# Two decoder layers on one core: the last of the eight squares of a norm kept beside the sum of the other seven, and added behind the transposes

## The chip, the cores and the metric

One core of a Trainium2 chip runs the whole program. The metric is the device time of one execution in microseconds. Lower is better.

## The reference, cut to what matters

Two layers of a decoder trunk work on x of 256 tokens by 1024 channels in float32. Each layer begins its two halves with an RMSNorm over the channels:

```python
def _rms(x, g):
    xf = x.astype(jnp.float32)
    y = xf * lax.rsqrt(jnp.mean(xf * xf, axis=-1, keepdims=True) + EPS)
    return (y * g.astype(jnp.float32)).astype(x.dtype)

xn = _rms(x, norm_mix_g);  z = einsum(xn, w_in)     # three mixers and their gates
x = x + einsum(merged, w_out)
xn = _rms(x, norm_ffn_g);  g, u = split(einsum(xn, w_gate_up))
x = x + einsum(silu(g) * u, w_down)
```

So there are four norms in the program: mixer and feed-forward of the first layer, then mixer and feed-forward of the second.

## The kernel before, in words

x lies transposed, as eight tiles x[0] to x[7] of 128 channels by 256 tokens. Every large product takes its operands as a sum of two parts, hi and lo (xg, fx, h, mg and y for activations, whi and wlo for weights), and is made of three matmuls (`feat`: hi by hi, hi by lo, lo by hi). The weights arrive in chunks of up to 128x1024 by DMA into raw. ScalarE makes whi from raw, VectorE makes wlo; there are three buffers of each.

`norm` does not scale x by its root mean square. It gives out the parts of x times the gain at once, and beside them the inverse root mean square in two shapes: rcol (tokens on the partitions) and rB (tokens along the free axis, the same on each partition). The products run on the unscaled parts, and their results are multiplied with rcol or rB when they leave PSUM. The PSUM tiles of the products (mm) have four buffers, those of all else (at) four more.

The sum of squares in `norm`, before: ScalarE squares x[0] into nacc and x[1] to x[7] into work tiles nsq, and GpSimd adds each nsq to nacc, seven adds in a row. In the first norm of the program, where x comes from memory, ScalarE squares all eight tiles into one wide tile sq and VectorE halves it three times (1024, 512 and 256 columns), the last time into nacc. Then two TensorE transposes (one for each half of the tokens, identity K1 as the moving operand) put nacc into a PSUM tile 128x2x128, VectorE reduces that over the channels to rcol (128x2), scales it and adds EPS, GpSimd takes the power -0.5 (rsqrt_cols), VectorE spreads rcol into rc, four transposes turn rc into PSUM, and ScalarE copies the result to rB. `S.gang()` keeps the transposes of a group together on TensorE and makes the first of them wait for all that the group needs.

The order of all instructions comes from a planner inside the kernel (`Order`). Every operation is recorded with a cost (`cost`, `lat`), and `Order.schedule` lays them out engine by engine in simulated time, by their place in the program and by when their inputs are ready. Each engine then runs its own list in that order. The costs that matter here:

```python
    if op.eng == "gpsimd":
        ...
        return 0.15 + n * 0.0021
```

and 0.2 us of latency to or from GpSimd. Work tiles (tag w) share 15 buffers. `Order.issue` first places the tags that PLACED names, in its order, with spaces in bytes between them; what follows nacc there (xg, y, h, w, mqk, K1) lies behind it in SBUF. In the trace every recorded instruction has the line 323 (`getattr(...)(*args, **kw)` in `Order.issue`), so instructions are told apart by their tiles.

Of the kernel before, what the change touches and what calls it, by code (L numbers as in the profile page):

```python
# [11 lines left out]
F32 = mybir.dt.float32  # L12
F32R = mybir.dt.float32r
BF16 = mybir.dt.bfloat16
AF = mybir.ActivationFunctionType
OP = mybir.AluOpType
AX = mybir.AxisListType.X
# [100 lines left out]
class Order:  # L118
# [191 lines left out]
    def issue(self):  # L310
        nc = self.tc.nc
        self.makespan = self.schedule()
        for tag in PLACED:
            if isinstance(tag, int):
# [79 lines left out]
T = 256  # L394
# [18 lines left out]
BR = (1, 2, 0)  # L413


PLACED = ("whi", "wlo", "nacc", 192, "xg", "y", "h", 192, "w", 224, "mqk", 192, "K1", 416)


def plan():
# [37 lines left out]
def kernel(ctx: ExitStack, tc: tile.TileContext, xT: bass.AP, wts: bass.AP, cst: bass.AP,  # L457
# [6 lines left out]
    S = Order(tc, sbuf, psum)  # L464
    V, A, G, PE, SP = (S.engine(n) for n in ("vector", "scalar", "gpsimd", "tensor", "sync"))

    def mmps(shape):
        return S.tile(shape, F32, tag="mm", name="mm", bufs=4, psum=True)

    def atps(shape):  # L470
        return S.tile(shape, F32, tag="at", name="at", bufs=4, psum=True)

    def tmp(shape, name="w"):
        return S.tile(shape, F32, tag="w", name=name, bufs=NW)
# [6 lines left out]
    K1 = S.tile([128, 256], F32, name="K1")  # L481
# [4 lines left out]
    x = [xs[:, 8 + k * T:8 + (k + 1) * T] for k in range(8)]  # L486
    ident, ones = K1[:, 0:128], K1[:, 128:256]
# [21 lines left out]
    def chunk(li):  # L509
        i = widx[0]  # L510
        widx[0] += 1
        w = WIDTH[i]
        raw = S.tile([128, CH], F32, tag="raw", name="raw", bufs=3)
        hi = S.tile([128, CH], F32R, tag="whi", name="whi", bufs=3)
        lo = S.tile([128, CH], F32R, tag="wlo", name="wlo", bufs=3)
        src = wts[li, OFFS[i]:OFFS[i + 1]].rearrange("(p c) -> p c", p=128)
        with S.early(600):
            if li == 0 and i < 2:
                return raw, hi, lo, src
            SP.dma_start(raw[:, :w], src)  # L520
            split(raw, hi, lo, 0, w)
        return hi, lo
# [20 lines left out]
    def rsqrt_cols(t, n):  # L543

        G.tensor_tensor(t, t, mhalf[:, :n], op=OP.pow)

    def gained(a, k, g):
        A.activation(a[:, 0, :], x[k], AF.Copy, scale=g)
        V.scalar_tensor_tensor(a[:, 1, :], x[k], g, a[:, 0, :].bitcast(F32), op0=OP.mult, op1=OP.subtract)

    def norm(gcol, wide, xg=None):

        first = xg is not None
        xg = xg or []
        acc = S.tile([128, T], F32, tag="nacc", name="nacc")
        for k in range(8 - len(xg)):
            g = gcol[:, k:k + 1]
            if not wide:
                a = S.tile([128, 2, T], F32R, tag="xg", name="xg", bufs=8)
            else:  # L560
                if k % 4 == 0:
                    y4 = S.tile([128, 4, 2, T], F32R, tag="y", name="fx", bufs=3)
                a = y4[:, k % 4]
            gained(a, k, g)
            xg.append(a)
        if first:
            sq = S.tile([128, 8 * T], F32, tag="y", name="sq8", bufs=3)
            with S.after(w_first[1][1]):
                for a in (0, 4 * T):
                    A.activation(sq[:, a:a + 4 * T], xs[:, 8 + a:8 + a + 4 * T], AF.Square)  # L570
            for n in (4 * T, 2 * T):
                V.tensor_add(sq[:, 0:n], sq[:, 0:n], sq[:, n:2 * n])
            V.tensor_add(acc, sq[:, 0:T], sq[:, T:2 * T])
        else:
            for k in range(8):
                if k == 0:
                    A.activation(acc, x[k], AF.Square)
                else:
                    sq = tmp([128, T], "nsq")
                    A.activation(sq, x[k], AF.Square)  # L580
                    G.tensor_add(acc, acc, sq)
        ps = atps([128, 2, 128])
        with S.gang():
            for t in range(2):
                PE.transpose(ps[:, t, :], acc[:, t * 128:(t + 1) * 128], ident)
        rcol = S.tile([128, 2], F32, tag="rcol", name="rcol", bufs=2)
        V.tensor_reduce(rcol, ps, axis=AX, op=OP.add)
        V.tensor_scalar(rcol, rcol, 1.0 / D, EPS, op0=OP.mult, op1=OP.add)
        rsqrt_cols(rcol, 2)
        rr = tmp([128, 2, 128], "rc")  # L590
        V.tensor_copy(rr, rcol[:, :, None].to_broadcast([128, 2, 128]))
        ps = atps([128, 2, T])
        with S.gang():
            for i in range(2):
                for t in range(2):
                    PE.transpose(ps[:, i, t * 128:(t + 1) * 128], rr[:, t, :], ident)
        rB = S.tile([128, T], F32, tag="rB", name="rB", bufs=2)
        A.activation(rB, ps[:, 0, :], AF.Copy)
        return xg, rcol, rB
# [161 lines left out]
    for li in range(L):  # L761
        widx[0] = 2 if li == 0 else 0
        c = col[li]
        r = row[li] = S.tile([128, R_N], F32, tag="row", name="row")
        ps_first = mmps([128, 2, T]) if li == 0 else None
        if li == 0:
            first_pair(ps_first)
        xg, rcol, rB = norm(c[:, C_NM:C_NM + 8], False, xg0 if li == 0 else None)
        if li:
            SP.dma_start(r, rows[li:li + 1, :].to_broadcast([128, R_N]))  # L770
# [6 lines left out]
        mqk = []  # L777
        for fp in range(4):
            if li == 0 and fp == 0:
                ps = ps_first  # L780
            else:
                ps = mmps([128, 2, T])
                for j in range(2):
                    w = chunk(li)
# [25 lines left out]
        ps = [mmps([128, 256]) for _ in range(2)]  # L810
        for a in range(2):
            w = chunk(li)
            for t in range(2):
                for kk in range(4):
                    k = 4 * a + kk
# [27 lines left out]
        for ks in ((0, 1, 2), (3, 4, 5), (6, 7)):  # L843
            w = chunk(li)
# [28 lines left out]
        for t in range(2):  # L873
            nk = 128 * (t + 1)
            m = mask1[:, 128:256] if t == 0 else mask1
            acc = tmp([128, 256], "isc")[:, :nk]
            ps = [atps([128, 2, nk]) for _ in range(2)]
# [5 lines left out]
            for j in range(2):  # L883
                p = ps[j]
                rl = tmp([128, 2, nk], "rl")
                A.activation(rl, p, AF.Relu)
                for hp in range(2):
                    h = 2 * hp + j
# [12 lines left out]
        def proj512():  # L901
            p = [mmps([128, 512]) for _ in range(2)]
            for a in range(4):
                w = chunk(li)
                for t in range(2):
                    for i in range(2):
                        k = 2 * a + i
                        tok(p[t], w, i * 512, 512, xg[k], t, k == 0, k == 7)
            return p

        sqT = S.tile([128, 4, T], F32, tag="qT", name="sqT", bufs=4)
        p = proj512()
# [5 lines left out]
        w = chunk(li)  # L918
        p = [mmps([128, 512]) for _ in range(2)]
# [4 lines left out]
        w = chunk(li)  # L924
        sv = []
        for t in range(2):
            p = mmps([128, 512])
# [5 lines left out]
        y = [S.tile([128, 4, 2, T], F32R, tag="y", name=f"y{b}", bufs=3) for b in range(3)]  # L933
        for t in range(2):
            yp = atps([128, 4, 128])
            n = 4 // (t + 1)
            for a in range(t + 1):
# [13 lines left out]
                with S.gang():  # L951
                    for i in range(n):
                        for kt in range(t + 1):
                            for j in range(2):
                                h = 2 * n * a + 2 * i + j
# [5 lines left out]
        p = tmp([128, 2, 64], "lamp")  # L961
# [11 lines left out]
        for j, dst in ((2, dqT), (3, dkT)):  # L973
            p = proj512()
# [4 lines left out]
        p = proj512()  # L979
        dv = [evac(p[t], rcol[:, t:t + 1]) for t in range(2)]  # L980
        for t in range(2):
            n = 4 // (t + 1)
# [4 lines left out]
            for hh in range(0, 4, n):  # L987
# [9 lines left out]
                a = tmp([128, nh, nk], "da")  # L997
# [4 lines left out]
                with S.gang():  # L1002
                    for i in range(nh):
                        h = hh + i
# [39 lines left out]
        with S.gang():  # L1044
            for t in range(2):
                p = atps([128, 4, 128])
# [21 lines left out]
        for t in range(2):  # L1068
            p = mB[t]
# [11 lines left out]
        for b, (si, ti) in enumerate(((0, 0), (1, 1), (0, 1))):  # L1081
            p = atps([128, 4, 128])
# [7 lines left out]
        p = proj512()  # L1090
# [7 lines left out]
        p = proj512()  # L1098
# [40 lines left out]
        for gp in range(12):  # L1139
            ps = mmps([128, 2, T])  # L1140
            for j in range(2):
                w = chunk(li)
# [13 lines left out]
        for n, b in enumerate(BR):  # L1156
            for ep in range(4):
                w = chunk(li)
                ps = mmps([128, 2, T])
# [9 lines left out]
                else:  # L1169
                    for j in range(2):  # L1170
                        V.tensor_add(us[ep][:, j, :], us[ep][:, j, :], u[:, j, :])
                        a = S.tile([128, 2, T], F32R, tag="xg", name="mg", bufs=8)
# [6 lines left out]
        for e in range(8):  # L1179
            w = chunk(li)  # L1180
            ps = mmps([128, T])
# [3 lines left out]


        xg, rcol, rB = norm(c[:, C_NF:C_NF + 8], True)
        hs = []
        for f in range(NFF):
            ps = mmps([128, 2, T])  # L1190
            for j in range(2):
                w = chunk(li)
# [7 lines left out]
            h = S.tile([128, 512], F32R, tag="h", name="h", bufs=22).rearrange("p (a t) -> p a t", a=2)  # L1200
# [3 lines left out]
        for e in range(8):  # L1204
            ps = mmps([128, T])
            for ks in (range(0, 8), range(8, 16), range(16, 22)):
                w = chunk(li)
# [76 lines left out]
```

## Time and profile before

| | us |
|---|---|
| runs, median of 3 | 909.11 |
| runs, lowest and highest | 903.57, 916.03 |
| profiled execution, own time | 910.13 |
| profiled execution, span of its instructions | 908.0 |

The profile is one execution seen by the hardware profiler. Its span goes from the first instruction to the last; the execution's own time is 2.13 us more. PE is TensorE's matmuls, PEld its weight loads, DVE VectorE, ACT ScalarE, POOL GpSimd, SP the queue that issues the DMAs. Matmuls overlap, so the duration of one is longer than the distance to the next: the distance (the pace) is a stretch's length over its count.

### The profile page before, as it was taken

The page shows a single profiled execution, that of the slowest core. Times are in us where ns is not written, and L with a number is a line of the kernel's source. Part 1 is how long each engine was busy: PE and PEld are TensorE (multiplying, and loading weights), DVE is VectorE, ACT ScalarE, POOL GpSimd, SP SyncE. Part 2 cuts the span into 40 slices and gives each one's busy share as a digit, 9 for nine tenths or more (in the row PEclk, how much of TensorE's full clock was granted, in tenths as well). Part 3 has the DMA queues.
Part 4 walks back from the last instruction along what each step waited for, and adds up shares of the span by engine and source line. Part 5 has one row for each costly group of instructions (what it writes and reads, how often), then busy time and mean ns, then how long its engine had stood idle before and what let it go on. Part 6 is the DMA issues. An engine that isn't in the chain of part 4 may idle for free.

```text
span 908.0 us, 18059 instructions
## 1 busy us (share of the span) xinstructions
PE 897.8 (99%) x7162; PEld 857.3 (94%) x7162; DVE 675.6 (74%) x1276; ACT 536.0 (59%) x928; POOL 111.6 (12%) x142
## 2 busy tenths in 40 slices
PE   9999999999999999999999999999999999999998
PEld 8978779999999999999999787899999999999998
DVE  6999989766896666665578899897669866666553
ACT  6786677765465444444457857687654655545442
POOL 0333342300021000000110221312000300000000
PEclk9999999999999999999999999999999999999999
DMA  8665524356555555555665554433555555555663
GB/s 260 197 200 183 165 91 126 123 176 196 196 187 186 187 186 187 186 176 189 190 188 181 181 186 141 138 110 125 186 190 194 198 185 191 197 195 189 197 210 102
DMA packets 46453, 160.50 MB, mean 177 GB/s; under 512 B 5408, under 2 KB 6560, under 8 KB 46368
## 3 DMA queue, kind: packets, MB, share of 16 engines
q1 hardware_dynamic: 46368, 159.34, 53.8%
q8 instruction: 56, 0.92, 0.4%
q14 instruction: 29, 0.24, 0.1%
HBM read 158.27 MB, written 1.05 MB: 175 GB/s over the span
## 4 chain that ended last, share of the span: by engine, by line
PE 88%; DVE 6%; POOL 2%; DMA 2%; issue 1%; ACT 1%; ACTq 0%; DVEq 0%
PE mm L323 83%; PE at L323 5%; DVE e L323 2%; DVE wlo L323 2%; POOL s L323 2%; DMA raw<-in_wts_dram 1%; ACT whi L323 1%; DMA x<-in_xT_dram 0%; DVE zr L323 0%; DVE cv L323 0%; DVE y L323 0%; DVE s L323 0%; DVE rot L323 0%; DVE pad L323 0%; DVE xg L323 0%
## 5 line engine op out<-in xcount | busy, mean ns | idle before, releaser
L323 ACT ACTIVATE whi<-raw 128x1024 fp32r<-128x1024 f32 (+3 forms) x304 | 316.5, 1042 | 316.6 <-PE mm L323 150.3
L323 DVE TENSOR_TENSOR wlo<-raw,whi 128x1024 fp32r<-128x1024 f32 (+3 forms) x304 | 364.5, 1200 | 170.8 <-ACT whi L323 169.0
L323 PE MATMUL mm<-fx,whi 128*128 128x256 f32 x1408 | 245.1, 279 | 0.0
L323 PEld LDWEIGHTS mm<-fx,whi 128*128 128x128 f32 x1408 | 214.7, 189 | 0.0
L323 PE MATMUL mm<-fx,wlo 128*128 128x256 f32 x704 | 195.9, 279 | 0.0
L323 PE MATMUL mm<-xg,whi 128*128 128x256 f32 x1024 | 181.4, 280 | 0.3 <-ACT whi L323 0.3
L323 PEld LDWEIGHTS mm<-xg,whi 128*128 128x128 f32 x1024 | 155.4, 188 | 1.7 <-issue 0.7
L323 PE MATMUL mm<-whi,xg 128*128 128x512 f32 (+2 forms) x512 | 149.1, 372 | 1.1 <-DVE pad L323 1.1
L323 PE MATMUL mm<-xg,wlo 128*128 128x256 f32 x512 | 142.5, 281 | 0.8 <-DVE wlo L323 0.8
L323 PEld LDWEIGHTS mm<-fx,wlo 128*128 128x128 f32 x704 | 132.0, 188 | 0.0
L323 PE MATMUL mm<-h,whi 128*128 128x256 f32 x704 | 122.1, 279 | 0.0
L323 PEld LDWEIGHTS mm<-whi,xg 128*128 128x128 f32 x512 | 92.0, 188 | 17.3 <-issue 1.5
L323 PEld LDWEIGHTS mm<-h,whi 128*128 128x128 f32 x704 | 107.4, 189 | 0.0
L323 PE MATMUL mm<-h,wlo 128*128 128x256 f32 x352 | 98.1, 279 | 0.0
L323 PEld LDWEIGHTS mm<-xg,wlo 128*128 128x128 f32 x512 | 95.8, 188 | 1.1 <-DVE wlo L323 1.1
L323 PE MATMUL mm<-wlo,xg 128*128 128x512 f32 (+2 forms) x256 | 94.9, 371 | 0.0
L323 PEld LDWEIGHTS mm<-h,wlo 128*128 128x128 f32 x352 | 66.1, 188 | 0.0
L323 PE MATMUL mm<-y,whi 128*128 128x256 f32 x384 | 65.4, 276 | 0.0
L323 POOL TENSOR_TENSOR nacc<-nacc,nsq 128x256 f32<-128x256 f32 x21 | 20.2, 962 | 348.0 <-ACT nsq L323 210.1
L323 PEld LDWEIGHTS mm<-y,whi 128*128 128x128 f32 x384 | 57.8, 188 | 0.0
L323 PEld LDWEIGHTS mm<-wlo,xg 128*128 128x128 f32 x256 | 48.1, 188 | 7.3
L323 PE MATMUL mm<-y,wlo 128*128 128x256 f32 x192 | 53.0, 276 | 0.0
(199 smaller groups left out, 1083.6 us busy)
## 6 DMA issues: line engine op xcount, KB each, us to landing
raw<-in_wts_dram SPq DMA_DIRECT2D x278, 512.0 KB, 3.4
raw<-in_wts_dram SPq DMA_DIRECT2D x16, 384.0 KB, 3.8
raw<-in_wts_dram SPq DMA_DIRECT2D x4, 498.0 KB, 4.0
raw<-in_wts_dram SPq DMA_DIRECT2D x4, 256.0 KB, 4.8
out_dram<-x SPq DMA_DIRECT2D x8, 128.0 KB, 3.4
row<-in_rows_dram SPq DMA_DIRECT2D x2, 388.0 KB, 5.3
x<-in_xT_dram SPq DMA_DIRECT2D x3, 256.0 KB, 5.0
raw<-in_wts_dram SPq DMA_DIRECT2D x2, 332.0 KB, 3.0
```

The source lines that it names most:

```text
L323: getattr(getattr(nc, o.eng), o.fn)(*args, **kw)
```

## The change

The eighth square is not added any more. A work tile `acc` of 128x2x256 takes the sum of squares 0 to 6 in its first half and square 7 in its second. In the first norm VectorE's second halving writes both halves of `acc` and the third halving is gone. Four transposes instead of two turn it into a PSUM tile 128x2x2x128, and VectorE's reduction runs over 2x128 columns for each of the two token halves. The tile nacc and its place in PLACED are gone.

```diff
-PLACED = ("whi", "wlo", "nacc", 192, "xg", "y", "h", 192, "w", 224, "mqk", 192, "K1", 416)
+PLACED = ("whi", "wlo", 192, "xg", "y", "h", 192, "w", 224, "mqk", 192, "K1", 416)
...
-        acc = S.tile([128, T], F32, tag="nacc", name="nacc")
+        acc = tmp([128, 2, T], "nacc")
...
-            for n in (4 * T, 2 * T):
-                V.tensor_add(sq[:, 0:n], sq[:, 0:n], sq[:, n:2 * n])
-            V.tensor_add(acc, sq[:, 0:T], sq[:, T:2 * T])
+            V.tensor_add(sq[:, 0:4 * T], sq[:, 0:4 * T], sq[:, 4 * T:8 * T])
+            V.tensor_add(acc.rearrange("p a t -> p (a t)"), sq[:, 0:2 * T], sq[:, 2 * T:4 * T])
         else:
             for k in range(8):
-                if k == 0:
-                    A.activation(acc, x[k], AF.Square)
+                if k in (0, 7):
+                    A.activation(acc[:, k // 7, :], x[k], AF.Square)
                 else:
                     sq = tmp([128, T], "nsq")
                     A.activation(sq, x[k], AF.Square)
-                    G.tensor_add(acc, acc, sq)
-        ps = atps([128, 2, 128])
+                    G.tensor_add(acc[:, 0, :], acc[:, 0, :], sq)
+        ps = atps([128, 2, 2, 128])
         with S.gang():
-            for t in range(2):
-                PE.transpose(ps[:, t, :], acc[:, t * 128:(t + 1) * 128], ident)
+            for i in range(2):
+                for t in range(2):
+                    PE.transpose(ps[:, t, i, :], acc[:, i, t * 128:(t + 1) * 128], ident)
         rcol = S.tile([128, 2], F32, tag="rcol", name="rcol", bufs=2)
-        V.tensor_reduce(rcol, ps, axis=AX, op=OP.add)
+        V.tensor_reduce(rcol, ps.rearrange("p t a c -> p t (a c)"), axis=AX, op=OP.add)
```

## Rows read from the trace of the kernel before

**Rows 1.** The head of the profile's page: the span, and each engine's busy time, its share of the span and its instructions.
```profile
span 908.0 us, 18059 instructions
PE 897.8 (99%) x7162; PEld 857.3 (94%) x7162; DVE 675.6 (74%) x1276; ACT 536.0 (59%) x928; POOL 111.6 (12%) x142
```

**Rows 2.** The chain of waits that ended last, in order of time: start, length in us, what, how many. The two stretches in which the chain leaves TensorE, first and last row of each.
```profile
109.34 1.14 DVE wlo L323
...
134.31 0.63 PE at L323 x4
...
560.47 1.14 DVE wlo L323
...
583.38 0.63 PE at L323 x4
```

**Rows 3.** The same chain: groups of transposes and other small matmuls (at) and the matmuls of the products (mm) right behind them.
```profile
176.17 1.78 PE at L323 x16
177.96 4.01 PE mm L323 x34
181.97 0.44 PE at L323 x4
182.40 6.59 PE mm L323 x58
189.00 0.44 PE at L323 x4
189.43 87.89 PE mm L323 x775
277.32 0.41 PE at L323 x2
277.74 3.42 PE mm L323 x29
281.15 0.44 PE at L323 x4
281.59 183.64 PE mm L323 x1558
465.45 3.19 PE mm L323 x27
...
628.15 1.78 PE at L323 x16
629.93 4.01 PE mm L323 x34
633.94 0.44 PE at L323 x4
634.38 8.52 PE mm L323 x75
642.90 0.44 PE at L323 x4
643.33 83.34 PE mm L323 x735
726.68 0.41 PE at L323 x2
727.09 3.42 PE mm L323 x29
730.51 0.44 PE at L323 x4
730.94 173.32 PE mm L323 x1529
```

**Rows 4.** The four long stretches of matmuls as windows: from and to, length, busy time and count of PE, PEld, DVE, ACT and POOL, then the granted clock, the DMAs' share and GB/s.
```profile
189.43:276.50 87.07, 87.07 (x771) 87.07 (x770) 67.48 (x90) 48.42 (x72) 6.32 (x7) 1.00 0.59 193
281.59:465.23 183.64, 183.64 (x1561) 183.56 (x1560) 113.32 (x159) 90.43 (x129) 6.02 (x7) 1.00 0.58 187
643.33:726.00 82.67, 82.67 (x732) 82.67 (x731) 64.86 (x88) 45.83 (x69) 6.53 (x7) 1.00 0.58 194
730.94:904.20 173.26, 173.26 (x1530) 173.11 (x1528) 104.83 (x144) 80.75 (x110) 0.00 (x0) 1.00 0.58 188
```

**Rows 5.** The end of the sum of squares in the first layer's feed-forward norm, instructions in order of time: start, us, engine, operation, out<-in, and in brackets the idle time before it and what ended it.
```profile
275.68 0.41 ACT L323 ACTIVATE nsq<-x 128x256 f32<-128x256 f32 x1
276.23 1.01 POOL L323 TENSOR_TENSOR nacc<-nacc,nsq 128x256 f32<-128x256 f32 x1 [1.72 <-ACT nsq L323]
277.29 0.20 PEld L323 LDWEIGHTS at<-K,nacc 128*128 128x128 f32 x2 [0.18 <-POOL nacc L323]
277.77 0.42 DVE L323 TENSOR_REDUCE rcol<-at 128x2 f32<-128x256 f32 x1 [0.25 <-PE at L323]
279.15 1.23 DVE L323 TENSOR_TENSOR wlo<-raw,whi 128x1024 fp32r<-128x1024 f32 x1 [0.75 <-ACT whi L323]
```

**Rows 6.** Who waited for the tile nacc over the whole program: waiter, us, times.
```profile
  PEld at L323: 0.4, 2
```

**Rows 7.** The first norm, instructions in order of time, as in rows 5.
```profile
18.07 0.42 DVE L323 TENSOR_TENSOR nacc<-sq 128x256 f32<-128x256 f32 x1
23.16 0.29 DVE L323 COPY rc<-rcol 128x256 f32<-128x256 f32 x1 [0.59 <-POOL rcol L323]
23.51 0.66 PE L323 MATMUL at<-K,rc 128*128 128x128 f32 x4 [0.39 <-DVE rc L323]
```

**Rows 8.** Groups of instructions of one shape on VectorE: out<-in, shapes, count, busy us, mean ns of one, idle us before.
```profile
L323 DVE TENSOR_REDUCE rcol<-at 128x2 f32<-128x256 f32 x4 | 1.7, 422 | 1.0 <-PE at L323 1.0
L323 DVE TENSOR_REDUCE m<-at 128x4 f32<-128x512 f32 x2 | 1.4, 682 | 0.0
```

**Rows 9.** By tile: durations in ns (least, median, most), first and last start in us. The last is a transpose from its start to its end.
```profile
L323 POOL TENSOR_TENSOR nacc<-nacc,nsq x21: 742/876/1573, 263.3 to 725.6; 128x256 f32<-128x256 f32 x21
L323 DVE SCALAR_TENSOR_TENSOR fx<-x,col,fx x16: 471/958/966, 263.2 to 725.9; 128x256 fp32r<-128x256 f32 x16
L323 PE MATMUL at<-K,nacc x8: 270/272/329, 18.6 to 726.8; 128*128 128x128 f32 x8
```

## The prediction

> **What bounds the kernel.** I read the head of the page first: TensorE is busy for 897.8 of 908.0 us [rows 1]. Matmuls overlap, so "busy" may hide a slow pace; the chain of waits comes next. The reader is to see there that from 134 us to 560 us and from 583 us to the end it stays on TensorE but for short pieces, and that two stretches, 109.3 to 134.3 us and 560.5 to 583.4 us, run through VectorE and GpSimd [rows 2]. All norms but the first lie where TensorE is the bound, so anything taken off GpSimd there pays only through what it does to TensorE.
>
> Then the pace, length over count, from the chain [rows 3]. The gate and output products of both layers run at 87.89/775 = 113.4 ns and 83.34/735 = 113.4 ns for one matmul. The feed-forward of the second layer runs at 173.32/1529 = 113.4 ns; that of the first, the same code with the same shapes, at 183.64/1558 = 117.9 ns. The windows of these four stretches show a granted clock of 1.00 in each, the 2.4 GHz level, and almost the same DMA share, 0.58 to 0.59 [rows 4]. So the slow stretch is neither the clock nor the memory. It costs 1558 x (117.87 - 113.35) ns = 7.0 us, more than everything the change touches directly.
>
> Where does a stretch get its pace? Behind a group of small matmuls, as the chain shows [rows 3]. Behind the groups of sixteen (177.96 and 629.93 us) it is 4.01/34 = 117.9 ns. Behind the six groups of four transposes that more than 50 matmuls of one width follow it was fast five times: 182.40 us (113.6), 189.43, 634.38 (113.6), 643.33 and 730.94 us; once, at 281.59 us, slow, and it stayed slow for 184 us. Behind the pairs of transposes of nacc it was slow: 3.42/29 = 117.9 at 277.74 and at 727.09 us, 3.19/27 = 118.1 at 465.45 us. I read this as two states of the matmul pipeline, drawn anew at each interruption. Why one or the other, the rows do not tell.
>
> **The change part by part.** The sum is made against the profiled execution: 910.13 us, of which 908.0 is span and 2.13 lies around it. The median of the runs, 909.11, is 1.0 us less.
>
> Transposes: two more in each of four norms. A group of four takes 0.44 us on the chain [rows 3], 0.11 each. Six of the eight stand where TensorE is the bound: 6 x 0.11 = +0.66 us. The two in the first norm come ahead of a wait of 0.39 us on TensorE for rc [rows 7] and are part of the chain that ends that wait, below.
>
> A rule of the Trainium skill speaks of a higher price. The durations of single transposes agree with it here: 270 to 329 ns from start to end [rows 9]. The page "TensorE: Matmul & The Clock Gate", section "Part 4: PE-mode transpose", gives about 275 ns for one in a kernel's context. By that price the six would be an estimated 1.65 us, and the sum 1 us higher than mine. I take the pace in a group, since TensorE is released after 0.11 us.
>
> The wait for nacc: TensorE's weight load stood 0.18 us for GpSimd's last add at 277.29 us [rows 5], 0.4 us in two norms together [rows 6]. With the change the last input is square 7, which ended at 275.68 + 0.41 = 276.09 us; the add ended at 277.24. The planner moves the group too: it counts that add as 0.15 + 256 x 0.0021 = 0.69 us and a latency of 0.2, so the group comes about 0.9 us earlier in TensorE's list, at some 276.2 us, still behind 276.09. The wait goes: -0.36 us. Behind it the group's results (reduction, power, rc) come earlier too, but the products have four PSUM buffers and do not wait for rB; nothing is gained there. If square 7 runs late, up to 0.36 of the wait stays.
>
> VectorE: the reduction over 512 instead of 256 columns. The nearest row is another reduction of 512 columns out of PSUM, 682 against 422 ns [rows 8]: +0.26 us in each norm. In the feed-forward norm VectorE stood 0.75 us idle right behind the reduction and its scaling, waiting for ScalarE [rows 5], and that covers it. Without this cover the next wlo is 0.26 us later, at most 0.8 us for three norms. In the first norm the third halving (0.42 us [rows 7]) goes, the reduction grows by 0.26 and the two transposes take 0.22: +0.06 us until rB. I take 0, with -0.2 to +0.3.
>
> GpSimd: three adds of 0.74 to 1.57 us [rows 9] go. GpSimd is busy 12% of the span [rows 1]: 0. VectorE's lo part of fx took 471 ns at least and 958 in the median [rows 9]; the long ones stand beside an add, as the last one after 276.23 does, so the last fx of each norm may come 0.48 us sooner. That, too, is off the chain.
>
> The work tile: acc holds one of 15 buffers for some 15 us in place of its own tile. Its buffer comes round after 14 others, six squares and rc among them, and by then it is free: 0. If the planner held a square back for it, at most one square of 0.41 us would be late.
>
> The order: the list of every engine behind the first norm is planned anew, from slightly other costs. The trace shows what two orders of one layer's code may differ by: the stretch off TensorE is 134.31 - 109.34 = 25.0 us in the first layer and 583.38 - 560.47 = 22.9 us in the second [rows 2]. I take 0 and keep 2 us to each side.
>
> The place: xg, y, h, w and mqk lie 1024 bytes lower. No row shows what that does. The bound is the pace itself: at 117.9 in all four stretches, or at 113.4.
>
> Sum of the direct costs: +0.66 - 0.36 + 0 = +0.3 us, between +0.1 and +1.8 us without the order. By itself that is 910.4 us: nothing that can be seen.
>
> **So the pace decides.** All four long stretches are begun anew behind groups of four, five sixths of which ended fast. In the feed-forward norms there is one more thing for the change: the pairs, which left the slow pace three times out of three, become groups of four without a wait, so the four transposes of rc find the pipeline fast already more often. All four fast by these counts: (5/6)^4 = 0.48. Then the 7.0 us of the first layer's feed-forward come back, and the time is 910.1 + 0.3 - 7.0 = 903.4 us. The lowest of the runs shown, 903.57, would be such an execution; 909.11 and 916.03 lie about one and two slow feed-forwards above it. That supports the reading, and it also says that slow ones are commoner than one in six. This is my forecast, with 0.45; its own range is 901 to 906.
>
> **Rivals.** (1) One long stretch stays slow, as in the profile: 910.4 us, or 903.4 + 775 x 4.5 ns = 906.9 if it is a gate stretch. For it: the median of the runs, 909.11. Against: five of six. 0.32. A special case of it is that there is nothing to draw, the pace being fixed by the columns. The Trainium skill says so in the page named above, section "Back-to-back issue gap": 256 columns give about 109 ns at the full clock. By that rule neither pace should be, the two would be a matter of the operands, and the sum stands at 910.4. The trace disagrees with it, since both paces occur with the same shapes at a granted clock of 1.00.
>
> (2) Slower: the wider group leaves the slow pace as the pairs did, and the four of rc do not undo it, as they did not at 281.59 us. Place: both feed-forwards. Price: the second layer's 1529 x 4.5 ns = 6.9 us on top of the first's. 910.4 + 6.9 = 917.3 us. It decides as soon as both run at 117.9. For it: 916.03 among the runs. Against: the group of four before 730.94. 0.13.
>
> (3) The new order or place weighs more than the norms: with all four long stretches slow, 903.4 + 7.0 + 6.9 + 3.5 + 3.3 = 924.1 us, plus 4 us for two worse orders, 928; the better side is 903.4 - 4 = 899. 0.10 over both signs. That the change does not do what it says, the eighth add staying in some way, the diff excludes.
>
> **How the numbers follow.** The forecast and the gate case of (1) lie under 907, the rest of (1) at 910.4, (2) at 917.3. A range from 900.5 to 917.5 leaves out some of (2) and most of (3), about 0.15 to 0.2. About 2% of the time, 18 us, is what a measurement of this kernel can tell from no change. Faster by that would be under 891, where no case reaches: 0.02. Slower would be over 927, only the end of (3): 0.04. Within: 0.94.
>
> **What would show it right or wrong.** Right: three groups of six adds on GpSimd; transposes of nacc sixteen in all; no wait of TensorE on GpSimd's nacc; the reduction at about 0.68 us; and the first layer's feed-forward at 113.4 ns. If that stretch has 117.9 ns and the time is about 910, (1) holds; if both have it, (2). Wrong would be a time that moves by more than the paces of the four long stretches explain, or a feed-forward whose pace changes midway without any group of small matmuls in it: then the pace is not drawn at the interruptions.

## The result, and the profile after

| | before | after |
|---|---|---|
| median, us | 909.65 | 902.61 |
| lowest and highest, us | 902.23 to 916.91 | 901.74 to 903.26 |
| executions near 903 / 910 / 916 us, of 21 | 6 / 9 / 6 | 21 / 0 / 0 |

The ratio is 0.994 (95% interval 0.9923 to 0.9957). It leaves out executions more than 1.5% above the fastest of their kernel, so the cluster near 916 us is not in it; by the medians the gain is 7.0 us.

The kernel before does not have one time but three, some 6.7 us apart, and after the change only the lowest is left. The lowest cluster itself hardly moved, from 903.0 us on average to 902.6. The profiled execution after took 902.09 us, span 900.3. The head of its page:

```profile
span 900.3 us, 18068 instructions
PE 891.1 (99%) x7170; PEld 851.3 (95%) x7170; DVE 675.1 (75%) x1275; ACT 535.9 (60%) x928; POOL 108.8 (12%) x139
```

The chain of waits after, the rows that answer to [rows 3]:

```profile
275.92 0.44 PE at L323 x4
276.35 2.64 PE mm L323 x23
278.99 0.44 PE at L323 x4
279.43 177.51 PE mm L323 x1566
456.94 0.44 PE at L323 x4
457.37 3.77 PE mm L323 x33
...
635.76 82.53 PE mm L323 x728
718.29 0.44 PE at L323 x4
718.73 2.62 PE mm L323 x23
721.35 0.44 PE at L323 x4
721.79 174.79 PE mm L323 x1542
```

The reader is to see that the first layer's feed-forward now runs at 177.51/1566 = 113.4 ns a matmul, where it had 117.9, and the second layer's still at 174.79/1542 = 113.4. Behind the groups of four for the sum of squares the pace is fast too (2.64/23 = 114.8, with the first, longer distance in it). The two feed-forwards as windows, columns as in [rows 4]: the clock is what it was, and the DMA share 0.61 and 0.59 beside 0.58.

```profile
279.43:456.90 177.47, 177.47 (x1568) 177.47 (x1568) 112.84 (x160) 91.23 (x129) 5.24 (x6) 1.00 0.61 193
721.79:896.50 174.71, 174.71 (x1542) 174.58 (x1541) 105.18 (x145) 81.49 (x110) 0.00 (x0) 1.00 0.59 187
```

The first feed-forward norm, columns as in [rows 5]: the last fx of the kernel before, then the kernel after.

```profile
276.56 0.96 DVE L323 SCALAR_TENSOR_TENSOR fx<-x,col,fx 128x256 fp32r<-128x256 f32 x1
...
275.10 0.40 ACT L323 ACTIVATE nacc<-x 128x256 f32<-128x256 f32 x1
275.66 0.45 PEld L323 LDWEIGHTS at<-K,nacc 128*128 128x128 f32 x4
275.98 0.48 DVE L323 SCALAR_TENSOR_TENSOR fx<-x,col,fx 128x256 fp32r<-128x256 f32 x1
276.39 0.69 DVE L323 TENSOR_REDUCE rcol<-at 128x2 f32<-128x512 f32 x1
```

TensorE no longer stands for GpSimd (the row has no bracket, where before it had 0.18 us), the last fx takes 0.48 instead of 0.96 us and has no add beside it any more, and the reduction takes 0.69. Over the program GpSimd makes 18 adds into nacc (three groups of six) and TensorE 16 transposes of it, as forecast.

### The profile page after: what moved, and what is told of

Its sections match the earlier page's. It is cut to its first block, busy times and chain, and to the rows that moved or that the text cites. A ratio compares the mean times of both kernels' runs of the same rounds, so it can differ in the third digit from the quotient of the medians.

```text
span 900.3 us, 18068 instructions
## 1 busy us (share of the span) xinstructions
PE 891.1 (99%) x7170; PEld 851.3 (95%) x7170; DVE 675.1 (75%) x1275; ACT 535.9 (60%) x928; POOL 108.8 (12%) x139
## 4 chain that ended last, share of the span: by engine, by line
PE 90%; DVE 6%; POOL 2%; ACT 1%; issue 1%; DMA 1%; SPq 0%; DVEq 0%
PE mm L323 85%; PE at L323 5%; DVE e L323 2%; DVE wlo L323 2%; POOL s L323 2%; DMA x<-in_xT_dram 1%; ACT whi L323 0%; DVE zr L323 0%; SPq L323 0%; DVE y L323 0%; DVE s L323 0%; ACT xg L323 0%; DVE rot L323 0%; DVE cv L323 0%; DVE mn L323 0%
## 5 line engine op out<-in xcount | busy, mean ns | idle before, releaser
L323 PE MATMUL mm<-fx,whi 128*128 128x256 f32 x1408 | 240.3, 276 | 0.0
L323 PEld LDWEIGHTS mm<-fx,whi 128*128 128x128 f32 x1408 | 212.2, 188 | 0.0
L323 PE MATMUL mm<-h,whi 128*128 128x256 f32 x704 | 119.8, 276 | 0.0
L323 POOL TENSOR_TENSOR nacc<-nacc,nsq 128x256 f32<-128x256 f32 x18 | 17.6, 978 | 331.5 <-ACT nsq L323 198.1
```

The lines of the kernel that those rows point to most:

```text
L323: getattr(getattr(nc, o.eng), o.fn)(*args, **kw)
```

## The experiments

Theory A was the prediction's: the wait ahead of the pair puts the matmuls into the slow pace, and the four transposes of rc draw between the paces only when they find them slow. Rivals were B (four transposes instead of two are what counts) and C (the place of the tiles in SBUF is). The kernel before ran beside each batch; its three clusters tell whether there was anything to draw on that chip. Counts are executions near 903 / 910 / 916 us, and each ratio is to the kernel before.

| kernel | executions | counts | median, us | ratio, 95% interval |
|---|---|---|---|---|
| before, first chip | 35 | 11 / 19 / 5 | 909.44 | |
| e1, four with wait | 12 | 12 / 0 / 0 | 904.41 | 0.998 (0.9954 to 1.0007) |
| e2, pair, no wait | 12 | 12 / 0 / 0 | 903.64 | 0.9953 (0.9926 to 0.998) |
| e3, place alone | 12 | 12 / 0 / 0 | 902.77 | 0.9961 (0.9936 to 0.9986) |
| e6, float32 group added | 12 | one cluster | 909.32 | 1.0028 (1.0002 to 1.0053) |
| before, second chip | 29 | 24 / 5 / 0 | 903.01 | |
| e4, after, old place | 12 | 12 / 0 / 0 | 902.64 | 0.9989 (0.9971 to 1.0006) |
| e5, planned later | 6 | 0 / 4 / 2 | 911.9 | 1.0107 (1.0067 to 1.0146) |
| e8, place up | 12 | 11 / 0 / 1 | 903.09 | 0.9989 (0.9968 to 1.001) |
| e9, identity moved | 12 | 11 / 1 / 0 | 902.55 | 0.9991 (0.9968 to 1.0015) |
| before, third chip | 35 | 5 / 19 / 11 | 909.66 | |
| e4b, as e4 | 12 | 12 / 0 / 0 | 902.43 | 0.9906 (0.9875 to 0.9937) |
| e10, sum tile elsewhere | 12 | 12 / 0 / 0 | 902.65 | 0.9919 (0.9887 to 0.9951) |
| e9b, as e9 | 12 | 2 / 5 / 5 | 909.79 | 0.998 (0.9933 to 1.0026) |
| e7, second group | 12 | 12 / 0 / 0 | 904.07 | 0.993 (0.9902 to 0.9959) |

**e1, four transposes with the wait.** The edit to the kernel before:

```diff
-        ps = atps([128, 2, 128])
+        ps = atps([128, 2, 2, 128])
...
-            for t in range(2):
-                PE.transpose(ps[:, t, :], acc[:, t * 128:(t + 1) * 128], ident)
+            for i in range(2):
+                for t in range(2):
+                    PE.transpose(ps[:, t, i, :], acc[:, t * 128:(t + 1) * 128], ident)
...
-        V.tensor_scalar(rcol, rcol, 1.0 / D, EPS, op0=OP.mult, op1=OP.add)
+        V.tensor_scalar(rcol, rcol, 0.5 / D, EPS, op0=OP.mult, op1=OP.add)
```

Expected: 

> The kernel before with nacc transposed twice over (four transposes, the reduction over 512 columns, the scale halved to fit); the seventh add and the wait for it stay. Theory A (the wait ahead of the transposes puts the matmuls into the slow pace, and a group of four that finds them slow draws between the two paces): times in three clusters as before, near 903, 910 and 917 us, a feed-forward slow in about half of the cases; median about 910. Theory B (a group of four, instead of a pair, sets the fast pace): all executions near 903 to 904 us, both feed-forwards at 113.4 ns. Theory C (the place of the tiles): as before, near 910.

All 12 executions lay between 903.38 and 905.54 us. The chain of e1 around the first feed-forward norm:

```profile
276.92 0.63 PE at L323 x4
277.54 3.31 PE mm L323 x29
280.85 0.44 PE at L323 x4
281.29 176.47 PE mm L323 x1557
```

The wait is in the first row (0.63 us for four), yet 3.31/29 = 114 and 176.47/1557 = 113.3 ns follow. So the wait does not condemn the stretch, against A. B's case came out, a little above its time: four transposes in the old place are enough for the feed-forwards. But for the added pair, TensorE's order in these two norms is that of before.

The median is 1.6 us above that of e3 on the same chip. Six more transposes are 0.66 us of it at the pace of a group. Another 0.8 us stands behind the group of rc of the second layer's mixer norm, which left the slow pace in the profile of e1 (first row) and the fast one in that of e3 (second row); at e3's pace 235 would take 28.6 us:

```profile
462.31 29.36 PE mm L323 x235
461.69 28.33 PE mm L323 x233
```

So four transposes did not end every draw: here, where rc waited and a shorter stretch follows, one was lost.

**e2, the pair without the wait.** The edit to the kernel after:

```diff
-        ps = atps([128, 2, 2, 128])
+        ps = atps([128, 2, 128])
...
-            for i in range(2):
-                for t in range(2):
-                    PE.transpose(ps[:, t, i, :], acc[:, i, t * 128:(t + 1) * 128], ident)
+            for t in range(2):
+                PE.transpose(ps[:, t, :], acc[:, 1, t * 128:(t + 1) * 128], ident)
...
-        V.tensor_reduce(rcol, ps.rearrange("p t a c -> p t (a c)"), axis=AX, op=OP.add)
+        V.tensor_reduce(rcol, ps, axis=AX, op=OP.add)
```

Expected: 

> The kernel after with only the half of the work tile that holds square 7 turned, by two transposes, and reduced over 256 columns; the sum of the other seven squares does not reach the norm. Theory A: no wait, so fast ahead of rc and fast behind it: all executions within 901 to 903.5 us, median about 902. Theory B: a pair sets nothing: three clusters, median about 909. Theory C: as after, 902.

901.98 to 904.11 us, so four are not necessary once the tile lies elsewhere and the wait is gone; this run does not separate the two. (The second layer's mixer norm lost its draw here too, 30.14 us for 242 matmuls behind rc at 459.88 us, about 0.8 of the 1.0 us that e2 lies above after.) In its trace the pair of the first layer was followed by the slow pace (2.72/23 = 118.3 ns) and the group of rc behind it by the fast one all the same:

```profile
276.10 2.72 PE mm L323 x23
278.82 0.44 PE at L323 x4
279.25 177.50 PE mm L323 x1566
```

**e3, the place alone.**

```diff
-PLACED = ("whi", "wlo", "nacc", 192, "xg", "y", "h", 192, "w", 224, "mqk", 192, "K1", 416)
+PLACED = ("whi", "wlo", 192, "xg", "y", "h", 192, "w", 224, "mqk", 192, "K1", 416)
```

Expected: 

> The kernel before with nacc taken out of PLACED, so that xg, y, h, w, mqk and K1 lie 1024 bytes lower as after; nothing else is changed. Theories A and B: three clusters as before, near 903, 910 and 917 us, median about 910. Theory C: all near 902 to 903 us.

In the traces every engine runs the same instructions in the same order as before; only addresses differ. All 12 lay between 902.35 and 903.33 us. This I had not expected: the arithmetic of the change is not needed for its gain.

**e6, an attempt to put the slow pace back.** Behind the four transposes of the kernel after:

```diff
+            if not first:
+                slow = atps([128, 2, 129])
+                for i in range(8):
+                    PE.matmul(slow[:, i % 2, :], acc[:, 0, 0:128], K1[:, 0:129], start=True, stop=True)
```

Expected: 

> The kernel after with eight float32 matmuls of 129 columns behind the four transposes of nacc in the last three norms; in both traces the groups of that shape (mv by ET) were followed by the slow pace each time. They take about 0.9 us a norm, 2.7 us in all. Theory A: the matmuls ahead of rc run at 117.9 ns, the four transposes of rc find them slow, and each feed-forward is drawn anew: three clusters near 905, 912 and 919 us, median about 912. Theories B and C (four transposes of rc set the fast pace by themselves, or the place does): all near 905 us.

One cluster, 908.94 to 909.82 us. The price was wrong: the trace counts each of these float32 matmuls twice, and the group takes 2.23 us instead of 0.44, 1.8 us a norm where I had 0.9. Three of these make 5.4 of the 6.7 us above after; most of the rest arose in the second layer's mixers. And the slow pace was not put back: seven matmuls stand between the added group and rc, and in the first layer's feed-forward norm the distances from one to the next are 200, 118, 122, 116, 114 and 113 ns, so rc found the fast pace, as it did in the other two norms. Behind rc it was fast too (179.32/1582 = 113.4). So e6 is no test of A; it shows that a group of this shape is not always followed by the slow pace.

**e4, after in the old place** (twice, since the second chip left nothing to tell apart):

```diff
-PLACED = ("whi", "wlo", 192, "xg", "y", "h", 192, "w", 224, "mqk", 192, "K1", 416)
+PLACED = ("whi", "wlo", 1024, 192, "xg", "y", "h", 192, "w", 224, "mqk", 192, "K1", 416)
```

Expected first: 

> The kernel after with 1024 bytes of space where nacc stood, so that xg, y, h, w, mqk and K1 lie where they lay before; the instructions and their order are those of after. Theory B (a group of four leaves the fast pace, so the groups of rc find it): all executions near 902 to 903.5 us. Theory C (the place alone removes the draw): three clusters near 903, 910 and 916 us, median about 909.

Expected the second time: 

> The kernel after in the old place once more, since the kernel before was slow in only 5 of 29 executions beside the first run of it (on another chip 41 of 59 were), which left nothing to tell apart. If the kernel before is drawn here about evenly: theory B (four transposes without a wait are enough) all near 902 to 903.5 us; theory C (the place alone does it) clusters near 903, 910 and 916 us.

On the third chip 901.49 to 903.06 us, beside 5 / 19 / 11 of the kernel before. The place of xg to K1 is not needed either. The sum of squares still lies in a work tile here, not where nacc was, and the order is that of after, so e4b does not separate the number of transposes, their tile and the order. (The 41 of 59 in its expectation counts three executions twice; the two sets hold 39 of 56.)

**e5, the pair planned later.**

```diff
-        return 0.15 + n * 0.0021
+        return 0.15 + n * (0.0040 if op.fn == "tensor_add" else 0.0021)
```

Expected: 

> The kernel before with the planner counting GpSimd's tensor_add of 256 columns at 1.17 us instead of 0.69, so that the pair of transposes of nacc is planned later (some three matmuls) and need not wait; place, sum and pair as before, though the order of other instructions changes with it. Theory A (the wait brings the slow pace, the groups of rc draw only if they find it): all near 902 to 903 us. Theories B and C: each feed-forward slow in about half of the executions, median about 909.

Against A: four executions near 911 and two near 918 us, on a chip where the kernel before was mostly near 903. The pair itself did not wait any more, but the new order made the group of rc wait (0.66 us for four), and behind it 184.23/1563 = 117.9 ns:

```profile
280.25 0.30 DVE rc L323
280.56 0.04 issue
280.60 0.66 PE at L323 x4
281.26 184.23 PE mm L323 x1563
...
731.48 0.66 PE at L323 x4
732.13 173.43 PE mm L323 x1530
```

The wait of rc does not decide either: in the second layer its group waited as long, and 173.43/1530 = 113.4 ns followed. Of the 9 us above the undrawn kernels, 7 are a slow feed-forward, the first layer's in the profile; by their times all six executions had one.

**e8, e9 and e10, which place.** Each is the kernel before with one edit to PLACED:

```diff
e8:  "wlo", "nacc", 192, "xg"  ->  "wlo", "nacc", 1216, "xg"
e9:  "mqk", 192, "K1"          ->  "mqk", 1216, "K1"
e10: "wlo", "nacc", 192, "xg"  ->  "wlo", 1216, "xg"
```

Expected of e8: 

> The kernel before with 1024 bytes more behind nacc: xg, y, h, w, mqk, K1 and the rest lie 1024 bytes higher, so that their distances from whi and wlo are those of after plus 2048. Nothing else is changed. Theory C1 (what counts is the distance to whi and wlo within 2048 bytes): all near 902.5 to 903.5 us, as in the run with the place alone. Theory C2 (what counts is the address as such, or the place of nacc): three clusters, median about 909, or anything between.

Expected of e9: 

> The kernel before with 1024 bytes more ahead of K1: only the identity that the transposes read, and the tiles behind it, move; weights, xg, y, h, w and mqk stay. Theory C3 (the identity's place sets how the transposes leave the pipeline): all near 902.5 to 903.5 us. Theory C1 (the operands of the products): three clusters near 903, 910 and 916 us, median about 909.

Expected of e9b: 

> The kernel before with K1 and the tiles behind it 1024 bytes higher, once more, for the same reason: 2 of 12 executions were above 904 us where 5 of 29 of the kernel before were. Theory C1: drawn like the kernel before beside it. Theory C3 (the identity's place): all near 902.5 us.

Expected of e10: 

> The kernel before with nacc taken out of PLACED and 1024 bytes of space left in its stead: nacc itself and the tiles placed after it move, while weights, xg, y, h, w, mqk and K1 stay where they lay. Theory C1 (the places of the products' operands): drawn like the kernel before beside it, clusters near 903, 910 and 916 us. Theory C4 (the place of nacc, that is, the transposes' own operand): all near 902.5 to 903.5 us.

e8 is undecided by its times, 11 of 12 near 903 us where 24 of 29 of the kernel before were. The one at 916.66 us has the profile, and it speaks against A once more. Behind the pairs of both feed-forward norms the pace was fast, and the groups of rc left the slow one:

```profile
277.42 0.41 PE at L323 x2
277.83 3.31 PE mm L323 x29
281.14 0.44 PE at L323 x4
281.58 183.64 PE mm L323 x1558
...
726.93 3.33 PE mm L323 x29
730.26 0.44 PE at L323 x4
730.70 180.10 PE mm L323 x1529
```

e9b was drawn like the kernel before, 2 / 5 / 5, so neither K1's place nor that of all tiles behind it matters by itself. e10 was not drawn: 902.18 to 903.42 us. It leaves weights, xg, y, h, w, mqk and K1 where they were, so of the theories C1 falls and C4 stands: with nacc itself somewhere else, the draw is gone. e10 also moves the tiles first used after nacc by 1024 bytes against the rest, and e3 does so too, as it lowers xg to K1. That remains as a second reading. e9b narrows it: there these tiles lie 1024 bytes further from the weights and from xg to mqk, and it was drawn, so what is left of it is their distance to K1 and to what lies between. All these places follow from the order of placing; no trace holds an address. The chain of e10:

```profile
277.05 0.42 PE at L323 x2
277.46 3.31 PE mm L323 x29
280.77 0.44 PE at L323 x4
281.21 176.49 PE mm L323 x1557
```

The profile of e9b is the plainest one against A: in the first layer the group of rc found the slow pace and left the fast one, in the second the other way round.

```profile
276.78 3.42 PE mm L323 x29
280.20 0.44 PE at L323 x4
280.64 176.48 PE mm L323 x1557
...
719.26 3.31 PE mm L323 x29
722.57 0.44 PE at L323 x4
723.00 180.10 PE mm L323 x1529
```

**e7, a second group of four.** Behind rB in the kernel before:

```diff
+        if not first:
+            again = atps([128, 2, T])
+            with S.gang(), S.after(rB):
+                for i in range(2):
+                    for t in range(2):
+                        PE.transpose(again[:, i, t * 128:(t + 1) * 128], rr[:, t, :], ident)
```

Expected: 

> The kernel before with four more transposes of rc, into a PSUM tile that nothing reads, some 20 matmuls behind those of rc in the last three norms; 1.3 us of TensorE. If each group of four is a draw of its own that only a slow pipeline can lose from, a feed-forward is slow as often as the square of the share in the kernel before (about 0.2 for 0.45). If each group is a draw whatever comes ahead, as often as in the kernel before (0.45). If the second group always sets the fast pace: all near 904 us.

903.48 to 904.99 us, all 12, 1.4 us above e10 beside it; the added transposes are 1.3 by their pace. In its profile both first groups of rc lost, with the fast pace ahead of them, and both second groups nine matmuls on restored it:

```profile
281.63 0.44 PE at L323 x4
282.07 1.07 PE mm L323 x9
283.13 0.44 PE at L323 x4
283.57 175.45 PE mm L323 x1548
...
725.33 1.07 PE mm L323 x9
726.40 0.44 PE at L323 x4
726.84 172.29 PE mm L323 x1520
```

1.07/9 = 118.9 ns between the groups, 175.45/1548 = 113.3 behind them. So a stretch does get its pace from the last interruption. Why the second group always won is not shown; it stood between other matmuls than the first, nine behind it and not the twenty of the expectation.

**What happens behind a group.** From the starts of the matmuls in the traces, the distances in ns that follow the last transpose of rc in the first layer's feed-forward norm (the first product matmul starts some 28 ns after the transpose; these come next):

```
before (stayed slow)   201 118 117 118 118 117 119 117 118
e10    (became fast)   201 117 118 122 118 114 113 113 114
e1     (fast at once)  206 116 114 113 113 114 113 113 114
```

Over the 14 traces, of the groups of two, four and eight transposes (identity moving) that at least ten matmuls of 256 columns follow, all 137 with a first distance of 204 to 208 ns were followed by the fast pace; of 165 with 199 to 203 ns, 103 were and 62 were not. A slip of some 5 ns, at once or a few matmuls later, is what separates a stretch at 113.4 from one at 117.9 ns. In each of the 103 the fast pace began within the first six distances, in none later: the pace is settled there.

## Why the prediction was right, and where its reasons were not

**The time.** 903.4 forecast, 902.61 measured. The term that carried it, 1558 x 4.52 ns = 7.0 us in the first layer's feed-forward, came back as read: 183.64 us for 1558 before, 177.51 for 1566 after. The three clusters, 902.7, 909.6 and 916.2 us on average over the 21 and the first 35 executions before, stand 6.9 and 6.6 us apart, as 7.0 and 6.9 had been worked out for the one and the other feed-forward.

**The direct sum.** +0.3 us forecast, between +0.1 and +1.8. Beside undrawn executions on the same chip it came out near -0.2, under the lower bound: 902.64 us for e4 beside 902.79, the median of the 24 executions of the kernel before near 903, and 902.43 for e4b beside 902.65 for e10. What the sum had wrong is a term that it took as fixed, the 2.13 us around the span. Every execution with its span on record has 2.07 to 2.20 us there if the kernel has the tile nacc, and 1.74 to 1.85 if the sum lies in a work tile. Why, no run shows. The spans themselves differ by less than 0.1 us on average in both pairs (900.8 and 900.7, 900.6 and 900.6). Within the span the parts are near the forecast: 0.44 us for a group of four, where a pair took 0.41 with its wait and 0.22 without (at 465.23 us), +0.28 over three norms; no wait for nacc; the reduction at 0.69 us. What takes the 0.2 to 0.3 us back, the runs do not resolve; the new order, which I took as 0, can hold it.

**The price of a transpose.** The Trainium skill's page "TensorE: Matmul & The Clock Gate", section "Part 4: PE-mode transpose", gives about 275 ns for one in a kernel's context. By that price the prediction's six would have been an estimated 1 us dearer. The runs side with the pace of a group: e7 has twelve transposes more than e10 beside it and came out 1.4 us later, 0.12 us each.

**The chances.** Here the step failed, though the case was the right one. I counted five fast stretches of six behind groups of four and took (5/6)^4 = 0.48 for all four stretches at the fast pace, as if all groups drew alike. They do not. Counting one slow feed-forward for each execution near 910 us and two near 916, the groups of rc in the kernel before lost 29 of 70 times on the first chip, 5 of 58 on the second and 41 of 70 on the third, those of the kernel after, e4 and e4b counted in, in none of 45 executions. A sixth was an average over groups that always win and one that often loses. So the forecast's case and its time were right, and that the change would bring it about was in part luck, as the reason given for it, next, does not hold.

**Why four instead of a pair should help.** I said that the groups of rc would find the pipeline fast already. e7 and e8 show groups that found it fast and lost, e2 one that found it slow and won. In the five profiles of kernels with the pair in its old place and the old order there (before, e7, e8, e9, e9b) the first group of rc in a feed-forward norm lost behind five of the six pairs that left the fast pace and behind one of the four that left the slow pace. So the pairs draw too, three pairs of three with the slow pace in the one profile were no rule, and what the sum's transposes hand on to those of rc is not the pace. That the change can end the feed-forwards' draw through the sum's transposes alone is shown for their number: four in the old place are enough (e1). Their tile elsewhere is enough too, with the pair and the order as before (e3, e10), if the second reading of e10 is left aside; the change does both, and so does e4b. By what way this reaches the group of rc 29 matmuls later is open.

**The rival of place.** I gave place and order together 0.10 and thought of it as a shift of all paces. Place was one of two sufficient causes, and the order, in e5, made things worse by 9 us against the undrawn kernel, 7 of them a slow feed-forward: both weighed more than I allowed. That all operands of the products moved by 1024 bytes, which had worried me, did nothing (e3 against e10).

**A rule that was to deny it.** The Trainium skill's page "TensorE: Matmul & The Clock Gate", section "Back-to-back issue gap", gives 262 cycles for 256 columns, about 109 ns at the full clock, as the gap of an isolated matmul; for a stream it says that weight loads and matmuls set the spacing together. So it denies the two paces less than the prediction said. The traces have one weight load for each matmul and two paces, 113.4 and 117.9 ns, at a granted clock of 1.00; the measurement decides.

## What to carry to other kernels

When executions of one kernel fall into clusters, look for stretches of the same code at different paces, and price the difference before any edit: here it was 7 us, where the direct effect of the change was near 0.2. A time that is drawn needs the kernel before on the same chip beside every run, since the odds themselves differed from one chip to the next. An edit that wins by ending a draw may owe it to a side effect: run the side effects (a tile's place, the number of instructions) one at a time.

## What the runs showed of the hardware that I had not expected

- The odds differed between the chips: the kernel before was near 903 us in 11 of 35 executions on the first, 24 of 29 on the second and 5 of 35 on the third. There was one batch on each, so what of this is the chip's and what the batch's is not shown.
- Where a 128x256 tile lies that two transposes read (or where the tiles first used after it lie) decides whether 1500 matmuls that do not read it may run 4% slow, with every engine's instructions and their order the same (e10: 12 / 0 / 0 beside 5 / 19 / 11).
- Once drawn, a pace holds: 1558 matmuls at 117.9 ns over 184 us with no change midway, until the next group of small matmuls. None of the 56 stretches of 728 matmuls or more in the 14 traces goes from one pace to the other on its way.
- What lies around the span is not fixed: 2.07 to 2.20 us with the tile nacc, 1.74 to 1.85 with the sum in a work tile.
